# A decoder layer on one core: turned blocks of the feed-forward issued in spaced steps, token-tile differences on GpSimd, attention values one item later, down splits inside the last pair

## The chip, the cores and the metric

The kernel runs on one core of a Trainium2 chip. The time is that of one execution on the device in microseconds (us). The core's engines run side by side, each through its own list of instructions in order: TensorE (PE) multiplies matrices, VectorE (DVE), ScalarE (ACT) and GpSimd (POOL) work on tiles, SyncE (SP) issues transfers. An instruction waits on semaphores for what it needs, and all behind it in its engine's list waits with it.

## The reference

One layer of a decoder over 1024 tokens of width 1024, all in fp32, with three parts, each followed by a layer norm of `ALPHA * x + f(x)`:

```python
h = hybrid_mixer(x, w_in, ml_conv_w, ...)     # mLSTM heads and sliding-window attention, one output projection
x = layer_norm(ALPHA * x + h, ln1_g, ln1_b)
h = memory_cross_attention(x, mem, xa_wq, xa_wkv, xa_wo)    # 4 heads, 256 memory tokens
x = layer_norm(ALPHA * x + h, ln2_g, ln2_b)
u = causal_dwconv(x @ w_up, conv_w, conv_b)                 # width 3
g, val = split(u, 2)
x = layer_norm(ALPHA * x + (gelu(g) * val) @ w_down, ln3_g, ln3_b)   # 2816 inner channels
```

The mixer's query and key channels pass a causal convolution of width 4 and a SiLU before the mLSTM. The sliding-window attention has 8 heads of 64 (4 to a key-value head), a window of 128 tokens, a bias by distance and a sink for each head.

## The kernel before

**Numbers.** Every fp32 operand of a product is held as two parts, a high (`whi`, `aA`, `pt[0]`; a copy that rounds, on ACT) and a low (the difference, on DVE or POOL). `mm3` (L146) makes a product of three matmuls: high times high, high times low, low times high (L147 to L149). Whoever makes the low last holds up the second or third matmul. `hi_lo` (L79) is the pair of copy and subtraction, `stage` (L120) the same for weights.

**Order.** The order on every engine is the order in which the program is written. Side work is written as generators: `also` (L52) opens one, each `yield us` asks to go on that many microseconds later on a clock of its own that `tick` moves by 0.68 us for each `mm3`, and `tick` (L62) issues what is due between two products. So steps of norms, attention and turns lie between the matmuls by these numbers. `drain` (L68) issues all that is left.

**The mixer** runs in two halves of 512 tokens. In each, `swa` (L489) walks 16 items (token tile by pair of heads) as side work of the projections: logits `lg` on PE (L442), bias and maximum on DVE (L450), the exponent on ACT (L458), normalisation on DVE (L467), then `swa_turn` (four transposes on PE into the PSUM tile `tp`, and the pair `pt` by `hi_lo`), then `swa_values` (six matmuls `pv`). Beside it run the projections of `qk`, whose convolution (`qk_steps`, L406) is on DVE too (L418, L424). The PSUM tiles `lg`, `tp`, `pv` come from one pool of 4 buffers, `mx`.

**Cross-attention.** `attend` is the side work for one head beside the next head's query projection (L854).

**The feed-forward** makes the up-projection of 22 pairs of blocks (128 gate and 128 value channels) with seven products P1 to P7 in place of eight, as Strassen does, on blocks of x turned to channels: B11 and B21 (first half of the tokens), B22, and the differences T1 to T4. `column_steps` (L902) works out, for one token tile of each half, norm and differences (L900) and turns them (L893); it runs as side work of the last columns of the `wo` projection and of the first products. `seq` (L944) is the order of the products: P1 and P2 of the first four pairs (they need B11 and B21 alone), then P6, the first that needs a difference. `slot_steps` loads, sums and splits the weight blocks (`block_hi`, `block_lo`) some slots ahead. `gated_steps` does convolution and gate of a pair (L1042 and L1054 on ACT, L1045 and L1057 on DVE) and writes it out on POOL's queue (L1058).

**The down-projection** loads weights and activations on SP's queue (L1135, L1137) and splits them (`down_split`, L1141); its first tiles are made before and between the last two up products.

Of the kernel before, what the change touches and what calls it, by code (L numbers as in the profile page):

```python
# [15 lines left out]
P = 128  # L16
# [12 lines left out]
def decoder_layer_kernel(ctx, tc, t, out):  # L29
# [90 lines left out]
    def stage(n):  # L120
        while nsplit[0] <= min(n, len(plan) - 1):
            i = nsplit[0]
            load(i + 1)
            raw, shape = raws.pop(i)
            w = raw.shape[1]
            _, pool, th, tl = pools.get(plan[i][1], pools["w"])
            hi = pool.tile([P, 1024], F32R, tag=th, name=th)
            lo = pool.tile([P, 1024], F32R, tag=tl, name=tl)
            hi, lo = hi[:, :w], lo[:, :w]
            for c in (slice(0, w // 2), slice(w // 2, w)) if i == 0 else (slice(0, w),):  # L130
                nc.scalar.copy(hi[:, c], raw[:, c])  # L131
            eng = nc.gpsimd if plan[i][0][0] == "w_cm" and plan[i][0][1] >= 5 else nc.vector
            eng.tensor_tensor(lo, in0=raw, in1=hi.bitcast(F32), op=SUB)  # L133
            if len(shape) == 3:
                hi, lo = [v.rearrange("p (a b) -> p a b", a=shape[1]) for v in (hi, lo)]
            ready[i] = (hi, lo)
            nsplit[0] += 1
# [332 lines left out]
    def swa_turn(h, tt, p, kb, L):  # L470
        tp = mx.tile([P, 2, 2, P], F32, tag="mx", name="tp")
        for m in range(kb, 2):
            for b in range(2):
                nc.tensor.transpose(tp[:, m, b, :], L[:, b, m * P:(m + 1) * P], ident)
        pt = [ta.tile([P, 2, 256], F32R, tag=f"pt{v}", name="pt", bufs=1) for v in range(2)]
        tv = tp.rearrange("p m a b -> p m (a b)")
# [12 lines left out]
    def swa(h, swq, us):  # L489
        items = [(h, tt, p) for tt in range(4) for p in (0, 2, 1, 3)]  # L490
        lg, turned = [], None
        for n in range(len(items) + 3):
            if turned:
                swa_values(*turned)
            turned = swa_turn(*lg.pop(0)[:5]) if n > 1 and lg else None
            if n >= len(items):
# [210 lines left out]
    swq = sw_proj(0, x)  # L707
    also(swa(0, swq, 3.35), 1.0)
    qk = qk_proj(0, x)
# [134 lines left out]
    def queries(xT):  # L844
        oT = Split(act2, "B")
        for hd in range(4):
            q2 = []
            for d in range(2):
# [4 lines left out]
                q2.append(q)  # L853
            also(attend(hd, q2, oT, 1.5), 0.7)  # L854
        return oT
# [33 lines left out]

    def turn(src, dst, tt):  # L890
        ps = mx.tile([P, 512], F32, tag="mx", name="tps")
        for k in range(4):
            nc.tensor.transpose(ps[:, k * P:(k + 1) * P], src[:, k * P:(k + 1) * P], ident)  # L893
        c = slice(tt * P, (tt + 1) * P)
        hi_lo(dst[0][:, :, c], dst[1][:, :, c], ps.rearrange("p (k c) -> p k c", k=4))

    K1, K2 = slice(0, 512), slice(512, 1024)

    def sub(dst, x, y):
        nc.vector.tensor_tensor(dst, in0=x, in1=y, op=SUB)  # L900

    def column_steps(tt):  # L902

        ya, yb = y_t[tt], y_t[4 + tt]
        yield from norm_steps(yb, ln, 0, 2.15, 2.6)
        nc.gpsimd.dma_start(x2d[4 + tt], yb)
        yield 3.4
        turn(yb[:, K2], B22, tt)
        yield 1.0
        sub(ya[:, K1], yb[:, K1], ya[:, K1])  # L910
        yield 0.8
        turn(ya[:, K1], T1, tt)
        yield 1.5
        sub(yb[:, K1], yb[:, K1], yb[:, K2])
        sub(yb[:, K2], yb[:, K2], ya[:, K1])
        yield 1.0
        turn(yb[:, K1], T3, tt)
        yield 0.8
        sub(ya[:, K2], ya[:, K2], yb[:, K2])
        turn(yb[:, K2], T2, tt)  # L920
        turned.append(tt)

    def last_cols():
# [3 lines left out]
        for tt in range(4):  # L927
# [11 lines left out]
            add_res(1, tt, 1, pss[tt])  # L939
            also(column_steps(tt))  # L940
            tick(0)
# [5 lines left out]
    for i in range(NFT):  # L947
        seq += [("P1" if i >= NB else "P6", i)]
        if i:
            seq += [("P4", i - 1), ("P3", i - 1)]  # L950
        seq += [("P2", i), ("P6", i)] if i >= NB else []
        seq += [("P5", i), ("P7", i)]
    seq += [("P4", NFT - 1), ("P3", NFT - 1)]
# [12 lines left out]
    for i in range(NFT):  # L966
        n = where["P6" if i < NB else "P1", i] - 4
        loads += [(n, i, "v"), (n, i, "g")]
# [11 lines left out]
    def sums_of(p, i):  # L980

        if p == "P6":
            s = sums[i] = act2.tile([P, 4, 512], F32, tag="B", name="ws")
            sub(s[:, 0], graw[i][:, K1], vraw[i][:, K1])
# [36 lines left out]
    slots = slot_steps()  # L1021
    turned = []
    last_cols()
# [36 lines left out]
    def run_slot(p, i):  # L1060
# [4 lines left out]
        if p == "P1":  # L1065
            st["c1"] = wide()
            st["b"] = bank(mo, "mo")
            product(p, i, st["b"], B11, True)
            nc.scalar.copy(st["c1"][:, K2 if early else K1], st["b"])
        elif p == "P2":  # L1070
# [37 lines left out]
    def last_turns():  # L1108
        for tt in range(4):
            while tt not in turned:  # L1110
                yield 0.7
            turn(y_t[tt][:, K2], T4, tt)
            yield 1.5

    next(slots)
    for n, (p, i) in enumerate(seq[:-2]):
        next(slots)
        if n == 0:
            T4 += parts(act2, "B", 8)
            also(last_turns(), 1.0)  # L1120
        if (p, i) == ("P6", 0):
            drain()
            park = wp.tile([P, 2, D], F32, tag="ln", name="park", bufs=1)
        run_slot(p, i)

# [59 lines left out]

    down_split(1)
    tile_mm(0, 0, (0, 1))
# [140 lines left out]
```

## Time and profile before

| what | value |
|---|---|
| median of 3 runs | 1458.34 us (1458.25 to 1459.07) |
| the profiled execution, its own time | 1457.32 us |
| its span, first to last instruction | 1455.5 us |
| granted TensorE clock, mean | 0.994 of full speed |
| busy: PE, DVE, ACT, POOL | 97%, 68%, 43%, 14% of the span |
| columns of turned blocks and first products, 734 to 800 us | PE busy 77% of the stretch |

A share of busy time is a mean over stages. PE is the bound nearly everywhere; what a stage can still win is its idle time on PE and the stretches in which the granted clock is 0.50 (1.2 in place of 2.4 GHz). In rows of the trace a pair `us, engine line op` gives a start or length, and the part in brackets the idle time before it and what ended it.

### The profile page before, as it was taken

What the parts mean: (1) busy time and instruction counts of PE and PEld (TensorE: products, weight loads), DVE (VectorE), ACT (ScalarE), POOL (GpSimd) and SP (SyncE); (2) the same over time, 40 slices, a digit from 0 to 9 for tenths busy, and PEclk for the clock granted to TensorE, in tenths of its full rate; (3) what the DMA queues carried; (4) which work ended last, traced back from release to release, by engine and by line L of the source; (5) the groups of instructions that cost most, each with busy time, mean ns of one, the idle gap of its engine ahead of it and who ended that gap; (6) DMA issues with size and microseconds to landing.
All of it is one profiled execution on the core that took longest, in us unless ns stands there. A gap on an engine that the chain in (4) does not pass through costs nothing.

```text
span 1455.5 us, 18114 instructions
## 1 busy us (share of the span) xinstructions
PE 1412.2 (97%) x6876; PEld 1169.0 (80%) x6876; DVE 984.0 (68%) x1614; ACT 627.2 (43%) x1079; POOL 197.9 (14%) x258
## 2 busy tenths in 40 slices
PE   9999999999999999999978999999999989999997
PEld 7779888888888978888856788888888868888886
DVE  6587666886675675486586887777777776336535
ACT  6455435564253443234343445544444444323420
POOL 3441014410212010031040000000000000002002
PEclk9999999999999999999999999999999999999999
DMA  7314213124264312232222222221222237525731
GB/s 243 120 48 145 73 53 99 47 78 147 75 219 128 116 58 88 86 116 73 72 101 73 85 90 87 87 83 60 76 87 87 88 115 267 172 83 177 279 94 58
DMA packets 47431, 157.73 MB, mean 108 GB/s; under 512 B 5437, under 2 KB 5845, under 8 KB 46704
## 3 DMA queue, kind: packets, MB, share of 16 engines
q1 hardware_dynamic: 42192, 137.54, 29.1%
q0 software_dynamic: 5152, 19.04, 3.5%
q8 instruction: 54, 0.88, 0.2%
q14 instruction: 33, 0.27, 0.1%
HBM read 136.62 MB, written 21.51 MB: 109 GB/s over the span
## 4 chain that ended last, share of the span: by engine, by line
PE 79%; DVE 13%; ACT 4%; issue 2%; POOL 1%; DMA 0%; SPq 0%; DVEq 0%; ACTq 0%; POOLq 0%
PE upp L147 15%; PE upp L149 15%; PE upp L148 15%; PE ps L149 9%; PE ps L147 9%; PE ps L148 9%; DVE cv L418 3%; DVE L L467 1%; DVE wlo L133 1%; PE tps L235 1%; ACT whi L131 1%; DVE y L228 1%; ACT L L458 1%; DVE L L450 1%; ACT pr L819 1%
## 5 line engine op out<-in xcount | busy, mean ns | idle before, releaser
L147 PE MATMUL upp<-xc,blk 128*128 128x512 f32 x440 | 174.1, 396 | 0.3 <-DVE uc L1036 0.3
L149 PE MATMUL upp<-xc,blk 128*128 128x512 f32 x440 | 174.0, 396 | 0.0
L148 PE MATMUL upp<-xc,blk 128*128 128x512 f32 x440 | 173.7, 395 | 0.0
L133 DVE TENSOR_TENSOR wlo<-raw,whi 128x1024 fp32r<-128x1024 f32 (+2 forms) x97 | 119.3, 1230 | 59.8 <-ACT whi L131 59.5
L131 ACT CAST whi<-raw 128x1024 fp32r<-128x1024 f32 (+3 forms) x114 | 114.2, 1001 | 81.2 <-PE ps L149 66.1
L147 PE MATMUL upp<-dw,ag 128*128 128x512 f32 (+1 forms) x357 | 140.2, 393 | 3.4 <-ACT dw L80 2.1
L148 PE MATMUL upp<-dw,ag 128*128 128x512 f32 (+1 forms) x357 | 139.6, 391 | 2.5 <-DVE dw L81 2.5
L149 PE MATMUL upp<-dw,ag 128*128 128x512 f32 (+1 forms) x357 | 139.5, 391 | 0.0
L147 PE MATMUL ps<-aA,whi 128*128 128x512 f32 x336 | 133.5, 397 | 0.3 <-DVE gat L337 0.3
L149 PE MATMUL ps<-aA,wlo 128*128 128x512 f32 x336 | 131.8, 392 | 0.2 <-POOL wlo L133 0.2
L148 PE MATMUL ps<-aA,whi 128*128 128x512 f32 x336 | 131.2, 390 | 0.0
L1045 DVE SCALAR_TENSOR_TENSOR uc<-uc,fconv 128x1023 f32<-128x1023 f32 x88 | 112.9, 1283 | 26.6 <-ACT uc L1042 25.0
L149 PEld LDWEIGHTS upp<-xc,blk 128*128 128x128 f32 x440 | 82.5, 187 | 20.8 <-DVE blk L900 0.4
L147 PEld LDWEIGHTS upp<-xc,blk 128*128 128x128 f32 x440 | 82.5, 188 | 20.3 <-issue 0.7
L148 PEld LDWEIGHTS upp<-xc,blk 128*128 128x128 f32 x440 | 82.4, 187 | 19.9
L147 PE MATMUL ps<-whi,aA 128*128 128x512 f32 (+2 forms) x256 | 91.4, 357 | 0.2 <-ACT aA L80 0.2
L81 DVE TENSOR_TENSOR ag<-araw,ag 128x512 fp32r<-128x512 f32 x44 | 31.4, 714 | 89.0 <-ACT ag L80 88.9
L149 PE MATMUL ps<-whi,aA 128*128 128x512 f32 (+2 forms) x256 | 89.9, 351 | 0.2 <-DVE aA L81 0.2
L148 PE MATMUL ps<-wlo,aA 128*128 128x512 f32 (+2 forms) x256 | 89.6, 350 | 0.0
L1036 DVE TENSOR_TENSOR uc<-upp,uc 128x512 f32<-128x512 f32 x66 | 45.5, 689 | 62.9 <-PE upp L149 62.8
L147 PEld LDWEIGHTS upp<-dw,ag 128*128 128x128 f32 x357 | 67.3, 188 | 18.8 <-ACT dw L80 2.6
L148 PEld LDWEIGHTS upp<-dw,ag 128*128 128x128 f32 x357 | 67.4, 189 | 18.2 <-DVE dw L81 3.2
(395 smaller groups left out, 3215.3 us busy)
## 6 DMA issues: line engine op xcount, KB each, us to landing
raw<-in_w_up SPq DMA_DIRECT2D x48, 512.0 KB, 3.8
raw<-in_w_down SPq DMA_DIRECT2D x44, 512.0 KB, 4.4
raw<-in_w_cm SPq DMA_DIRECT2D x26, 512.0 KB, 3.7
ad<-uc POOLq DMA_DIRECT2D x22, 512.0 KB, 5.2
araw<-ad SPq DMA_DIRECT2D x44, 256.0 KB, 3.5
raw<-in_w_out SPq DMA_DIRECT2D x16, 512.0 KB, 4.2
raw<-in_wq SPq DMA_DIRECT2D x16, 512.0 KB, 3.6
raw<-in_wo SPq DMA_DIRECT2D x16, 512.0 KB, 3.6
```

The lines of the kernel that those rows point to most:

```text
L81: nc.vector.tensor_tensor(lo, in0=src, in1=hi.bitcast(F32), op=SUB)
L131: nc.scalar.copy(hi[:, c], raw[:, c])
L133: eng.tensor_tensor(lo, in0=raw, in1=hi.bitcast(F32), op=SUB)
L147: nc.tensor.matmul(ps, lhsT=ahi, rhs=bhi, start=start, stop=False, skip_group_check=more)
L148: nc.tensor.matmul(ps, lhsT=ahi, rhs=blo, start=False, stop=False, skip_group_check=more)
L149: nc.tensor.matmul(ps, lhsT=alo, rhs=bhi, start=False, stop=stop, skip_group_check=more)
L228: nc.vector.scalar_tensor_tensor(y, in0=y, scalar=rs[:, 0:1], in1=ln[:, 0, :], op0=MUL, op1=MUL)
L235: nc.tensor.transpose(ps[:, k * P:(k + 1) * P], y[:, kk * P:(kk + 1) * P], ident)
L418: nc.vector.scalar_tensor_tensor(cv, in0=xc[:, j:j + 512], scalar=mlc[:, i, j:j + 1], in1=cv, op0=MUL, op1=ADD)
L450: nc.vector.tensor_tensor_reduce(L[:, b, kb * P:256], in0=lv[:, b, :], in1=btab[:, i, kb * P:], scale=-1.0, scalar=nsnk[:, i:i + 1], op0=A ...
L1036: nc.vector.tensor_tensor(dst, in0=ps, in1=y, op=ADD)
L1045: nc.vector.scalar_tensor_tensor(u[:, d:S], in0=x[:, 0:S - d], scalar=fconv[:, i, 2 - d:3 - d], in1=u[:, d:S], op0=MUL, op1=ADD)
```

## The change

- `stage`: the lows of the 16 qk weight tiles (eight in each half) are made on DVE instead of POOL.
- `swa`: `pt` has two buffers, `turned` holds up to two items, and the values of an item are issued two items behind its turn, not one. The first half's attention starts 1 us later.
- `attend`'s steps are 2.0 us apart instead of 1.5.
- `turn` is a generator: transposes, 0.8 us later ACT's copy, 0.8 us later DVE's subtraction, with at most two open; before, all three were issued together.
- `column_steps`: the four differences of a token tile (16 in all) go from DVE to POOL, the first of them ahead of the turn of B22, and the write of the normed tile `yb` to `x2d` from POOL's queue to SP's.
- A P1 of the first four pairs issues all of that token tile's column steps behind its product, before the copy of its result. P5 of the first pair comes before its P6, and the rest of the column steps before P5, the turns of T4 before P4.
- In the last pair, the first down weights are loaded at P6 and split at P5, the second at P7; before, both were split behind the loop.
- The scratch for descriptors of transfers on POOL's queue is halved.

```diff
-            eng = nc.gpsimd if plan[i][0][0] == "w_cm" and plan[i][0][1] >= 5 else nc.vector
-            eng.tensor_tensor(lo, in0=raw, in1=hi.bitcast(F32), op=SUB)
+            nc.vector.tensor_tensor(lo, in0=raw, in1=hi.bitcast(F32), op=SUB)
...
-        pt = [ta.tile([P, 2, 256], F32R, tag=f"pt{v}", name="pt", bufs=1) for v in range(2)]
+        pt = [ta.tile([P, 2, 256], F32R, tag=f"pt{v}", name="pt", bufs=2) for v in range(2)]
...
-        lg, turned = [], None
-        for n in range(len(items) + 3):
-            if turned:
-                swa_values(*turned)
-            turned = swa_turn(*lg.pop(0)[:5]) if n > 1 and lg else None
+        lg, turned = [], []
+        for n in range(len(items) + 4):
+            if len(turned) == 2 or n == len(items) + 3:
+                swa_values(*turned.pop(0))
+            if n > 1 and lg:
+                turned.append(swa_turn(*lg.pop(0)[:5]))
...
-    also(swa(0, swq, 3.35), 1.0)
+    also(swa(0, swq, 3.35), 2.0)
...
-            also(attend(hd, q2, oT, 1.5), 0.7)
+            also(attend(hd, q2, oT, 2.0), 0.7)
...
-    def turn(src, dst, tt):
+    def turn(src, dst, tt, us=0.8):
+
+        while opened[0] == 2:
+            yield 0.3
+        opened[0] += 1
         ps = mx.tile([P, 512], F32, tag="mx", name="tps")
...
-        hi_lo(dst[0][:, :, c], dst[1][:, :, c], ps.rearrange("p (k c) -> p k c", k=4))
+        pv = ps.rearrange("p (k c) -> p k c", k=4)
+        yield us
+        nc.scalar.copy(dst[0][:, :, c], pv)
+        yield us
+        nc.vector.tensor_tensor(dst[1][:, :, c], in0=pv, in1=dst[0][:, :, c].bitcast(F32), op=SUB)
+        opened[0] -= 1
...
-        nc.gpsimd.dma_start(x2d[4 + tt], yb)
+        sub(ya[:, K1], yb[:, K1], ya[:, K1], nc.gpsimd)
         yield 3.4
-        turn(yb[:, K2], B22, tt)
-        yield 1.0
-        sub(ya[:, K1], yb[:, K1], ya[:, K1])
-        yield 0.8
-        turn(ya[:, K1], T1, tt)
+        nc.sync.dma_start(x2d[4 + tt], yb)
+        yield from turn(yb[:, K2], B22, tt)
+        sub(yb[:, K1], yb[:, K1], yb[:, K2], nc.gpsimd)
+        yield 0.5
+        yield from turn(ya[:, K1], T1, tt)
+        sub(yb[:, K2], yb[:, K2], ya[:, K1], nc.gpsimd)
         yield 1.5
-        sub(yb[:, K1], yb[:, K1], yb[:, K2])
-        sub(yb[:, K2], yb[:, K2], ya[:, K1])
-        yield 1.0
-        turn(yb[:, K1], T3, tt)
-        yield 0.8
-        sub(ya[:, K2], ya[:, K2], yb[:, K2])
-        turn(yb[:, K2], T2, tt)
+        yield from turn(yb[:, K1], T3, tt)
+        sub(ya[:, K2], ya[:, K2], yb[:, K2], nc.gpsimd)
+        yield from turn(yb[:, K2], T2, tt)
...
-            also(column_steps(tt))
+            columns.append(also(column_steps(tt)))
...
-        seq += [("P1" if i >= NB else "P6", i)]
+        seq += [("P1", i)] if i >= NB else [("P5", i), ("P6", i)] if i == 0 else [("P6", i)]
...
-            st["c1"] = wide()
             st["b"] = bank(mo, "mo")
             product(p, i, st["b"], B11, True)
+            if early:
+                drain(columns[i])
+            st["c1"] = wide()
             nc.scalar.copy(st["c1"][:, K2 if early else K1], st["b"])
...
+        if (p, i) == ("P5", 0):
+            drain(*columns)
+        if (p, i) == ("P4", 0):
+            drain(turns)
...
+        if i == NFT - 1 and p in ("P6", "P5", "P7"):
+            down_load(0) if p == "P6" else down_split(0 if p == "P5" else 1)
+
...
-    nc = _bacc.Bacc("TRN2", target_bir_lowering=False, num_devices=1, dynamic_dma_scratch_size=8192)
+    nc = _bacc.Bacc("TRN2", target_bir_lowering=False, num_devices=1, dynamic_dma_scratch_size=4096)
```

How the instructions stand in the engines' lists, at three places (a number behind a name tells one tile from another of that name).

PE in the first half's attention, before. `pt_1272` and `pt_1273` are high and low of the turn made one item earlier:

```order
L147 MATMUL pv_1314<-pt_1272,swv0_111 128x256
L148 MATMUL pv_1314<-pt_1273,swv0_111 128x256
L149 MATMUL pv_1314<-pt_1272,swv1_112 128x256
L474 MATMUL tp_1322<-ident_117,L_1209 128x128 x4
L442 MATMUL lg_1331<-kk0_107,swq_355 128x256
L443 MATMUL lg_1331<-klo0_109,swq_355 128x256
```

The same place after the change, where that turn's pair is called `pt_1271` and `pt_1272`, and `pt_1200` and `pt_1201` are of the turn before it:

```order
L146 MATMUL pv_1312<-pt_1200,swv0_111 128x256
L147 MATMUL pv_1312<-pt_1201,swv0_111 128x256
L148 MATMUL pv_1312<-pt_1200,swv1_112 128x256
L473 MATMUL tp_1320<-ident_117,L_1209 128x128 x4
L441 MATMUL lg_1329<-kk0_107,swq_355 128x256
L442 MATMUL lg_1329<-klo0_109,swq_355 128x256
```

The values read the older pair; transposes and logits behind them stand as they did.

DVE beside the qk projection of the first half, one item and the convolution of one block, before (L424 and L418 are the convolution, L461, L467 and L81 the attention's normalisation and `pt` low):

```order
L424 SCALAR_TENSOR_TENSOR qk<-th,cv 128x512
L461 RECIPROCAL ssum<-ssum 128x2
L467 TENSOR_SCALAR L<-L,ssum 128x128 x2
L418 SCALAR_TENSOR_TENSOR cv<-xc,mlc,cv 128x512 x2
L81 TENSOR_TENSOR pt<-tp,pt 128x256
```

And after, a line lower in the numbers:

```order
L423 SCALAR_TENSOR_TENSOR qk<-th,cv 128x512
L132 TENSOR_TENSOR wlo<-raw,whi 128x1024
L417 SCALAR_TENSOR_TENSOR cv<-xc,mlc,cv 128x512 x2
L460 RECIPROCAL ssum<-ssum 128x2
L466 TENSOR_SCALAR L<-L,ssum 128x128 x2
L417 SCALAR_TENSOR_TENSOR cv<-xc,mlc,cv 128x512
L81 TENSOR_TENSOR pt<-tp,pt 128x256
```

A weight low of 128x1024 has come in ahead of the item's steps.

POOL at the end of the column steps, before (`rs` are steps of the norm, L229 its last step, L906 the write to `x2d`, L1058 that of the gated pairs):

```order
L212 TENSOR_TENSOR rs<-mv,eps_c 128x1
L213 TENSOR_TENSOR rs<-rs,mhalf 128x1
L229 TENSOR_TENSOR y<-y,ln 128x1024
L906 DMA x2d<-y 128x1024
L1058 DMA ad<-uc 128x1024 x22
```

And after, where L228 is the norm's last step and L909 the differences:

```order
L909 TENSOR_TENSOR y<-y 128x512
L211 TENSOR_TENSOR rs<-mv,eps_c 128x1
L212 TENSOR_TENSOR rs<-rs,mhalf 128x1
L909 TENSOR_TENSOR y<-y 128x512 x3
L228 TENSOR_TENSOR y<-y,ln 128x1024
L909 TENSOR_TENSOR y<-y 128x512 x8
L1066 DMA ad<-uc 128x1024 x22
```

Eight of the sixteen differences stand behind the last tile's norm, four between the last two norms; no write to `x2d` is left on this queue here.

## Rows read from the trace of the kernel before

**Rows 1.** The page, busy us of each engine and its share of the span.

```profile
PE 1412.2 (97%) x6876; PEld 1169.0 (80%) x6876; DVE 984.0 (68%) x1614; ACT 627.2 (43%) x1079; POOL 197.9 (14%) x258
```

**Rows 2.** Waits of PE: us in total, times, longest us.

```profile
PE tps L893 <- DVE y L900: 9.4, 4, 4.8
PE pv L148 <- DVE pt L81: 9.2, 10, 1.9
PE upp L147 <- ACT uc L1069: 2.9, 4, 0.8
PE upp L149 <- DVE blk L900: 2.6, 1, 2.6
PE upp L148 <- DVE dw L81: 2.5, 1, 2.5
PE upp L147 <- ACT dw L80: 2.1, 1, 2.1
PE xtp L831 <- DVE pr L825: 1.9, 3, 1.1
```

**Rows 3.** Windows: us; busy PE, PEld, DVE, ACT, POOL; granted clock, DMA share, GB/s.

```profile
40.00:122.00 82.00, 75.40 (x398) 63.70 (x397) 63.28 (x138) 43.62 (x105) 35.44 (x47) 1.00 0.23 71
...
734.00:800.00 66.00, 50.86 (x238) 39.40 (x237) 46.42 (x72) 26.23 (x45) 12.05 (x10) 0.95 0.25 88
```

**Rows 4.** Windows of the three stretches at half clock, columns as above.

```profile
267.00:270.30 3.30, 3.30 (x15) 3.15 (x15) 3.09 (x10) 3.12 (x8) 1.36 (x3) 0.50 0.00 0
...
758.50:765.20 6.70, 5.78 (x17) 4.30 (x17) 3.94 (x7) 1.21 (x3) 0.74 (x2) 0.50 0.20 78
...
1195.40:1198.70 3.30, 2.78 (x7) 2.20 (x8) 2.21 (x3) 0.00 (x0) 0.00 (x0) 0.50 1.01 319
```

**Rows 5.** Timeline, 56 to 75 us: start, length, engine, line, operation.

```profile
60.40 2.39 POOL L133 TENSOR_TENSOR wlo<-raw,whi 128x1024 fp32r<-128x1024 f32 x1
...
60.46 3.67 DVE L418 SCALAR_TENSOR_TENSOR cv<-xc,mlc,cv 128x512 f32<-128x512 f32 x2 [0.46 <-POOL cv L413]
...
64.63 0.75 DVE L418 SCALAR_TENSOR_TENSOR cv<-xc,mlc,cv 128x512 f32<-128x512 f32 x1
```

**Rows 6.** Timeline of DVE, 711 to 714 us: a weight low on DVE.

```profile
712.06 1.23 DVE L133 TENSOR_TENSOR wlo<-raw,whi 128x1024 fp32r<-128x1024 f32 x1 [0.39 <-ACT whi L131]
```

**Rows 7.** Timeline of PE, 291 to 294 us: values, then the next logits.

```profile
292.79 0.38 PE L148 MATMUL pv<-pt,swv 128*128 128x256 f32 x1 [1.10 <-DVE pt L81]
...
293.84 0.36 PE L442 MATMUL lg<-kk,swq 128*128 128x256 f32 x1
```

**Rows 8.** Timeline of PE, 785 to 789 us: the first product of a turned block.

```profile
788.08 0.40 PE L147 MATMUL upp<-xc,blk 128*128 128x512 f32 x1
```

**Rows 9.** Timeline of POOL, 712 to 800 us: norm steps of the columns.

```profile
727.40 2.40 POOL L229 TENSOR_TENSOR y<-y,ln 128x1024 f32<-128x1024 f32 x1 [5.97 <-DVE y L228]
...
730.99 0.56 POOL L213 TENSOR_TENSOR rs<-rs,mhalf 128x1 f32<-128x1 f32 x1
```

**Rows 10.** Groups of POOL by line and form: busy us, mean ns, idle before.

```profile
L632 POOL TENSOR_TENSOR ht<-hn,ht 128x512 f32<-128x512 f32 x8 | 11.3, 1417 | 16.9 <-DVE hn L630 16.9
```

**Rows 11.** Timeline of DVE, 727 to 800 us: two differences.

```profile
732.44 0.68 DVE L900 TENSOR_TENSOR y<-y 128x512 f32<-128x512 f32 x1
...
756.37 2.83 DVE L900 TENSOR_TENSOR y<-y 128x512 f32<-128x512 f32 x1
```

**Rows 12.** Timelines of DVE, ACT and SP, 1170 to 1200 us.

```profile
1172.73 0.43 SPq L1135 DMA_DIRECT2D raw<-in_w_down  x1
...
1187.93 1.23 ACT L1042 ACTIVATE uc<-uc,fconv 128x1024 f32<-128x1024 f32 x1
...
1189.19 2.61 DVE L1045 SCALAR_TENSOR_TENSOR uc<-uc,fconv 128x1023 f32<-128x1023 f32 x2 [1.72 <-ACT uc L1042]
```

**Rows 13.** The tile of the bias table: its transfer's issue, its first reader.

```profile
L450 DVE CUSTOM_DVE_ANT_0 L<-lg,btab,nsnk x64: 343/476/486, 54.9 to 334.2; 128x256 f32<-128x256 f32 x56, 128x128 f32<-128x128 f32 x8
L693 POOL DMA_DIRECT2D btab<-ud x1: 942/942/942, 33.4 to 33.4; - x1
```

More of the change, by code (lines that the diff above doesn't have):

```diff
@@ L894, in turn, with sub @@
         c = slice(tt * P, (tt + 1) * P)
-        hi_lo(dst[0][:, :, c], dst[1][:, :, c], ps.rearrange("p (k c) -> p k c", k=4))
+        pv = ps.rearrange("p (k c) -> p k c", k=4)
[4 more added lines that the diff above has]
+        opened[0] -= 1
     K1, K2 = slice(0, 512), slice(512, 1024)
-    def sub(dst, x, y):
-        nc.vector.tensor_tensor(dst, in0=x, in1=y, op=SUB)
+    def sub(dst, x, y, eng=nc.vector):
+        eng.tensor_tensor(dst, in0=x, in1=y, op=SUB)
     def column_steps(tt):
@@ L951, in decoder_layer_kernel @@
         seq += [("P2", i), ("P6", i)] if i >= NB else []
-        seq += [("P5", i), ("P7", i)]
+        seq += [("P5", i), ("P7", i)] if i else [("P7", i)]
     seq += [("P4", NFT - 1), ("P3", NFT - 1)]
@@ L966, in decoder_layer_kernel @@
     for i in range(NFT):
-        n = where["P6" if i < NB else "P1", i] - 4
+        n = (where["P1", i] if i >= NB else min(where["P5", i], where["P6", i])) - 4
         loads += [(n, i, "v"), (n, i, "g")]
@@ L980, in sums_of @@
     def sums_of(p, i):
+        if p in ("P5", "P6") and i not in sums:
+            sums[i] = act2.tile([P, 4, 512], F32, tag="B", name="ws")
         if p == "P6":
-            s = sums[i] = act2.tile([P, 4, 512], F32, tag="B", name="ws")
+            s = sums[i]
             sub(s[:, 0], graw[i][:, K1], vraw[i][:, K1])
@@ L1021, in decoder_layer_kernel @@
     slots = slot_steps()
-    turned = []
+    turned, columns, opened = [], [], [0]
     last_cols()
@@ L1111, in last_turns @@
                 yield 0.7
[L1112 to L1124, printed above, removed]
+            yield from turn(y_t[tt][:, K2], T4, tt)
+            yield 0.5
     order = [(h, j) for h in range(2) for j in range(NFT)]
@@ L1184, in tile_mm @@
                 down_mm(banks[h, tt, ch], h, j, tt, ch, j == 0, j == NFT - 1)
-    down_split(1)
+    next(slots)
+    for n, (p, i) in enumerate(seq[:-2]):
+        next(slots)
+        if n == 0:
+            T4 += parts(act2, "B", 8)
+            turns = also(last_turns(), 1.0)
+        if (p, i) == ("P5", 0):
+            drain(*columns)
+        if (p, i) == ("P4", 0):
+            drain(turns)
+        if (p, i) == ("P6", 0):
+            park = wp.tile([P, 2, D], F32, tag="ln", name="park", bufs=1)
+        run_slot(p, i)
+        if i == NFT - 1 and p in ("P6", "P5", "P7"):
+            down_load(0) if p == "P6" else down_split(0 if p == "P5" else 1)
     tile_mm(0, 0, (0, 1))
```

## The prediction

> **What bounds the kernel now.** First the page's line of busy time: TensorE (PE) works 1412.2 us [rows 1] of a span of 1455.5. That leaves 43.3 us of idle PE, 1.2 of it ahead of the first matmul and 7.1 behind the last. The change takes no matmul away, so all that it can win lies in the other 35 us, and in what runs at half clock. Next, PE's list of waits [rows 2], which says who ends the idle time: 9.2 us in ten waits of the attention values (`pv`) for the `pt` lows; 9.4, 2.9 and 2.6 us around the column turns; 2.1 and 2.5 us ahead of the first down product; 1.9 us in the cross-attention. Then the windows by stage, to see what else is full there: in the first attention stretch DVE is busy for 63.3 of 82 us, so that a delay on it reaches PE; from 734 to 800 us PE works only 50.9 of 66 us [rows 3]. Last the granted clock: three short windows at 0.50, which is the 1.2 GHz level, each right behind such a wait of PE. What runs in them takes twice its time, so each costs half of PE's busy time there: 3.30/2 = 1.7, 5.78/2 = 2.9 and 2.78/2 = 1.4 us [rows 4].
>
> **The lows of the qk weights (POOL to DVE).** While POOL runs a `wlo` (2.39 us from 60.40), a pair of DVE instructions that starts 0.06 us later takes 3.67 us; a single one of the same kind, later and undisturbed, takes 0.75 [rows 5]. So one of the two waited out the POOL instruction, a loss of up to 2.1 us. The Trainium skill ("SBUF — State Buffer", section "SBUF: two separate sides") says why: DVE and GpSimd share a pair of ports, which an instruction of the one keeps to its end against one of the other with two SBUF inputs; this trace agrees, with 3.67 us for a pair at 0.75 each. After the change the hold is gone, but DVE carries the instruction: 1.23 us [rows 6], some 1.13 net since the next one starts about 0.1 us before its end. Eight per half make 9.0 us; eight holds of 0 to 2.1 us cost it 0 to 16.8. In the middle the two are equal, so I count no gain and no loss of DVE time, but the worst single delay falls from 2.1 to 1.13 us.
>
> **Attention values one item later.** PE does not escape the wait altogether. The next item's logits go to the PSUM buffer of the transposes whose `pt` low the values waited for, so they wait for the same DVE instruction. They stand only the values' other matmuls and four transposes later: 293.84 - 292.79 = 1.05 us [rows 7] for a full item, some 0.5 us for the first four items, which have half the matmuls. What a wait has above that is kept: 0.9 us of the longest, 1.9 [rows 2], and some 3 us of the 9.2 when added up over the ten, if the lows come as late as now. If they come 1 us earlier (2.1 less 1.13) nothing is left; if the new DVE work falls ahead of them where there was no hold, all stays. I take the middle of the first two, 1.5 left: 9.2 - 1.5 = **7.7** gained (0 to 9.2), and the half-clock window behind the longest of these waits, **1.7** (0 to 1.7).
>
> **Cross-attention.** A head's steps come 2.0 instead of 1.5 us apart, so the probabilities, for which PE waits up to 1.1 us [rows 2], have 0.5 us more at each of several steps: **1.6** of 1.9 us (0 to 1.9). The last head then ends closer to the output projection; I count nothing for it.
>
> **The column stretch.** This ends for PE with the first product of a fully turned block, at 788.08 [rows 8]. Of the time before, PE idles 66 - 50.9 = 15.1 us [rows 3] and loses 2.9 to the clock [rows 4], 18.0 together. After the change I leave of it:
> - 2.6 us, the wait for the first split block [rows 2]: what stands ahead of that block on DVE stays.
> - 4.8 us: the four copies of P1 now stand on ACT behind the copy of a turn, and PE must turn first. 1.2 us each, a choice; now they cost 0.7 each (2.9 in four).
> - 1.4 us for turns that find a difference not ready, a choice.
> That is 8.8, and 18.0 - 8.8 = **9.2** is gained; the product starts at 778.9. It supposes that the long waits of turns for `y` go, since a turn no longer stands ahead of products that are ready.
>
> What could hold this up is POOL. Its chain starts at 727.40: four L229 of 2.40, three pairs of small steps, whose longer one takes 0.56 [rows 9] and which I put at 0.84 a pair, and sixteen differences of p us. I add 8 us, a choice: 5 for DVE instructions let in between and for the last write of `yb`, which now stands on SP behind weight loads and must have landed before `yb` is overwritten, and 3 from the last difference through turn, copy and subtraction. So the product starts no earlier than 727.4 + 9.6 + 2.5 + 8 + 16p = 747.5 + 16p. The nearest row is POOL's own 128x512 fp32 instruction of two inputs, 1.42 us in the mean [rows 10]: 770.2, not the bound. POOL is the bound from p = 1.96, and at 2.54 the whole 9.2 is gone. A difference on DVE took 0.68 us alone and 2.83 held by an L229 [rows 11]; I take 1.42 as the same engine, shape and type, and 2.83 as the dear end. The bounds of the term: 18.0 less the 2.6 that stay, 15.4, and at p = 2.83 a product at 792.8, a loss of 4.7.
>
> Against this edit speaks the Trainium skill ("GPSIMD Engine Reference", section "4.1 Engine selection"): an elementwise instruction of two inputs belongs on VectorE, as GpSimd takes about twice the time. That makes p an estimated 1.36 us, by which the sum would be the same: the trace agrees (1.42 against 0.68), and the twofold price is paid on an engine for which PE hardly waits.
>
> **Down.** The first pair's weights are loaded a slot or more ahead (1172.73) but split only behind the last slot. Now their split comes earlier: ACT does both highs right behind L1042 (1187.93 + 1.23 = 1189.2, and 0.5 and 1.05 more: 1190.7, when the last product ends); DVE does both lows behind L1045 (1189.19 + 2.61 = 1191.8, and 0.6 and 1.22 more: 1193.6) [rows 12]. The first matmul, of the highs, then follows at once; the second waits for the low, about 2.6 us in place of 2.1 + 2.5: a gain of 2.0. What is pushed back on DVE by 1.8 us, a block's low and an update of `uc`, is needed behind some three microseconds of down matmuls that cover it; uncovered it would cost those 1.8. Behind one wait instead of two the clock may hold, which is worth 1.4: I take 0.9 of it. **2.9** (0.2 to 6.0, with no wait left).
>
> **At nothing.** Half the DMA scratch: the bias table, fetched by POOL's queue at 33.4 us, is first read at 54.9 [rows 13], a cover of 21.5 us for its landing; what it were later than that it would cost.
>
> **Sum.** 7.7 + 1.7 + 1.6 + 9.2 + 2.9 = 23.1 us. The profiled execution took 1457.3 us, which makes 1434.2; the median of the runs is 1.0 above it: **1435.2 us**.
>
> **Rivals.**
> - *The attention waits stay.* DVE, already 77% busy, gets 9 us more per half, and a `wlo` stands ahead of a `pt` low in most items. For: the order on DVE shows one just so. Against: rows 5, the longer hold ends. 1458.3 - (23.1 - 9.4) = 1444.6. Chance 0.11.
> - *POOL bounds the columns.* The differences wait for DVE's work of two SBUF inputs as DVE waited for POOL's, p near 2.5, the term zero: 1458.3 - 13.9 = 1444.4. The Trainium skill's rule on GpSimd bears on this one: no run here shows p. Chance 0.11; with the rival above, 1453.8, another 0.03.
> - *Slower.* The same mechanism turns the sign when the product starts 13.9 us late, at 802: p = (802 - 747.5)/16 = 3.4. At p = 3.6 it starts at 805.1, 17 us late: 1458.3 - 13.9 + 17 = 1461.4. For: a POOL instruction of 2.4 us holds DVE for 2.1, so the two can lock each other. Against: no DVE instruction there is as long as 2 us. Chance 0.06.
> - *Everything hides.* No attention wait, none in cross-attention, columns 15.4, down 6.0: 1458.3 - 9.2 - 1.7 - 1.9 - 15.4 - 6.0 = 1424.1. Chance 0.04.
> - *It does not do what it says*: the waits only change their names (logits for values, copies for turns), and the time stays at 1458. Chance 0.04.
>
> The forecast has 0.61. Half of each term's distance to its bounds, added in squares, gives it a range of its own from 1432 to 1443; to hold 8 in 10 the range takes in the first two rivals above and as much below, towards the case in which everything hides: **1427 to 1446**. That leaves out 0.17. Less than 0.2%, 2.9 us, can't be told from no change. Faster 0.90, the same 0.04, slower 0.06.
>
> **What would show it.** Right: no wait of `pv` for `pt`, and at most some 1.5 us of `lg` for it; differences on POOL of 1.3 to 1.5 us; no wait of 2 us or more between the first split block and the first product of turned columns, and four short ones for the copies of P1; one wait of some 2.6 us ahead of the down products, for a low on DVE; full clock near 267 and 758 us. Wrong: waits of `lg` of a microsecond and more in many items; PE waiting for POOL's differences; half clock in new places; DVE instructions of 2 us beside POOL's; a new wait between the last head of cross-attention and its output projection.

## The result, and the profile after

The changed kernel took 1440.73 us (median of four, 1437.31 to 1442.26) beside 1458.7 us for the kernel before, timed again with it: the ratio is 0.9871, 95% interval 0.9852 to 0.9891. The forecast was 1435.2 with a range of 1427 to 1446, so the direction and the range held and the gain came out at 18 us instead of 23. The profiled execution took 1440.82 us; its span is 1439.0 and PE is busy 1406.8 us of it.

PE's list of waits in the changed kernel (us in total, times, longest us), to be set beside [rows 2]:

```profile
PE upp L146 <- ACT uc L1079: 8.4, 4, 4.8
PE upp L148 <- DVE blk L909: 3.1, 1, 3.1
PE upp L147 <- DVE dw L81: 3.1, 2, 2.4
PE lg L441 <- DVE pt L81: 2.8, 5, 0.7
PE upp L146 <- DVE park L1044: 0.9, 1, 0.9
PE tps L897 <- POOL y L909: 0.7, 1, 0.7
PE tp L473 <- DVE L L466: 0.7, 2, 0.5
PE xtp L831 <- DVE pr L825: 0.3, 1, 0.3
```

No `pv` waits for a `pt` low any more; the logits do, for 2.8 us where the values waited 9.2, and no stretch at half clock is left near 267 us. The turns' long waits for `y` are gone. But the copy of P1 (`uc`, L1079), for which PE waited 2.9 us in four, now costs 8.4, and one of the four is 4.8 us long. The windows (columns as in [rows 3]) show two of the three stretches at half clock still there:

```profile
40.00:122.00 82.00, 79.36 (x426) 68.71 (x425) 66.29 (x155) 46.42 (x110) 20.25 (x40) 1.00 0.24 75
...
718.00:785.00 67.00, 53.71 (x261) 42.85 (x260) 44.65 (x61) 27.60 (x48) 33.68 (x26) 0.97 0.32 103
739.10:742.50 3.40, 3.40 (x11) 2.74 (x11) 2.48 (x3) 0.87 (x2) 1.01 (x2) 0.50 0.95 277
1179.40:1182.90 3.50, 3.50 (x10) 2.67 (x10) 2.79 (x4) 0.00 (x0) 0.53 (x1) 0.51 0.94 345
```

Where the time came from is read best by the start of one and the same matmul in both traces:

| matmul | before | after | earlier by | gained since the row above |
|---|---|---|---|---|
| first one behind the gates (waits for `gat`) | 18.43 | 19.03 | -0.6 | |
| gates' transpose, end of the first half's attention (L510) | 243.17 | 239.15 | 4.0 | 4.6 |
| first one with `memT`, after the second half's | 472.46 | 463.70 | 8.8 | 4.7 |
| first one with `gr`, last columns of `wo` | 715.84 | 704.20 | 11.6 | 2.9 |
| the one that waits 0.34 us for `uc`, behind the columns | 828.03 | 812.61 | 15.4 | 3.8 |
| the last one that waits for `y`, down | 1446.37 | 1429.61 | 16.8 | 1.3 |

The attention stretches gained 9.4 us, as the sum said; cross-attention 2.9 (1.6 expected); the column stretch 3.8 (9.2 expected); down 1.3: the two waits of 2.14 and 2.45 us at the split became one of 2.42, and 0.7 us were lost again at 1324 us, to a weight low that came after ACT had waited for a transfer.

The prediction measured the columns by another end, the first product of a fully turned block. Its start, behind the start of the first `gr` matmul, is the time to compare. Before, then after:

```profile
715.84 0.39 PE L147 MATMUL ps<-gr,aB 128*128 128x512 f32 x1
788.08 0.40 PE L147 MATMUL upp<-xc,blk 128*128 128x512 f32 x1
```

```profile
704.20 0.40 PE L146 MATMUL ps<-gr,aB 128*128 128x512 f32 x1
771.49 0.40 PE L146 MATMUL upp<-xc,blk 128*128 128x512 f32 x1
```

That is 72.24 and 67.29 us: 4.95 gained. Below, this time is called the column time.

The 4.8 us wait has one place. POOL's timeline in the changed kernel, up to the first P1:

```profile
718.23 1.29 POOL L909 TENSOR_TENSOR y<-y 128x512 f32<-128x512 f32 x1
...
726.21 3.49 POOL L909 TENSOR_TENSOR y<-y 128x512 f32<-128x512 f32 x2
729.66 2.84 POOL L228 TENSOR_TENSOR y<-y,ln 128x1024 f32<-128x1024 f32 x1
732.58 1.64 POOL L909 TENSOR_TENSOR y<-y 128x512 f32<-128x512 f32 x1
...
735.41 4.16 POOL L909 TENSOR_TENSOR y<-y 128x512 f32<-128x512 f32 x3
```

The timeline of all engines there, with ACT's copy and PE behind it:

```profile
738.38 0.59 ACT L1079 COPY uc<-upp 128x512 f32<-128x512 f32 x1 [3.58 <-POOL y L909]
...
739.02 0.72 PE L146 MATMUL upp<-aA,blk 128*128 128x512 f32 x1 [4.84 <-ACT uc L1079]
```

The copy's destination takes the buffer of the normed tile `yb` of the first token tile (both are tiles of one pool of eight), so it must wait until all readers of `yb` are done, and the one that ends last is the fourth difference, `ya -= yb`. It stands on POOL behind a norm step and differences of the tiles that follow. P2 adds to P1's PSUM bank, so PE waits for the copy. The price of a difference was close to what I took:

```profile
L909 POOL TENSOR_TENSOR y<-y 128x512 f32<-128x512 f32 x16 | 23.1, 1459 | 8.3 <-DMA x2d<-y 7.8
```

1.46 us in the mean (1.42 taken). The row also shows POOL waiting 7.8 us for the write of the last tile's `yb`.

### The profile page after: what moved, and what is told of

Read it like the earlier page. It is cut to its first block, busy times and chain, and to the rows that moved or that the text cites. A ratio compares the mean times of both kernels' runs of the same rounds, so it can differ in the third digit from the quotient of the medians.

```text
span 1439.0 us, 18150 instructions
## 1 busy us (share of the span) xinstructions
PE 1406.8 (98%) x6876; PEld 1169.1 (81%) x6876; DVE 977.0 (68%) x1614; ACT 626.8 (44%) x1079; POOL 188.9 (13%) x254
## 5 line engine op out<-in xcount | busy, mean ns | idle before, releaser
L132 DVE TENSOR_TENSOR wlo<-raw,whi 128x1024 fp32r<-128x1024 f32 (+2 forms) x113 | 139.4, 1233 | 59.5 <-ACT whi L131 58.8
L81 DVE TENSOR_TENSOR ag<-araw,ag 128x512 fp32r<-128x512 f32 x44 | 31.4, 713 | 87.8 <-ACT ag L80 87.8
L147 PEld LDWEIGHTS upp<-dw,ag 128*128 128x128 f32 x357 | 67.3, 188 | 18.8 <-DVE dw L81 3.8
```

The costliest lines, as they stand in the source:

```text
L81: nc.vector.tensor_tensor(lo, in0=src, in1=hi.bitcast(F32), op=SUB)
L132: nc.vector.tensor_tensor(lo, in0=raw, in1=hi.bitcast(F32), op=SUB)
L147: nc.tensor.matmul(ps, lhsT=ahi, rhs=blo, start=False, stop=False, skip_group_check=more)
```

## The experiments

Every run was timed against the kernel before on the same chip; the ratios are to that. The changed kernel is at 0.987.

### The changed kernel once more

No edit. 

> The changed kernel itself once more, since its four executions lie 4.9 us apart and those of the kernel before 2.3. If the spread is in the half-clock stretches or in the order in which DVE and POOL take turns, one execution here differs from another in the column stretch (first wait of P2 for the copy, 4.84 us in the trace so far) and nowhere else. If it is in transfers, the waits behind the second half of the down projection differ. Median 1440.7, between 1439 and 1442.

1440.4 us (1439.66 to 1442.01), ratio 0.9870 [0.9857, 0.9884]. In this profiled execution of 1442.0 us the wait for the copy is 2.75 us instead of 4.84, but two windows at half clock lie in the column stretch instead of one:

```profile
732.80:736.20 3.40, 3.40 (x14) 2.81 (x13) 3.33 (x6) 1.63 (x2) 3.32 (x3) 0.50 0.22 30
739.60:743.00 3.40, 2.83 (x7) 2.15 (x8) 2.29 (x4) 1.53 (x3) 1.58 (x1) 0.50 0.35 99
```

From the first `gr` matmul to the wait for `uc` this execution is 0.4 us faster all the same. It had lost 1.7 us before, in the first attention half (L510 starts at 240.86 instead of 239.15), where I had expected no difference. So the spread has more than one source, and a single trace's whole time says little below 2 us. The wait for the first copy belongs to this spread: in the six profiled executions that leave the columns as changed (these two and those of four runs below) it is 4.84, 2.75, 1.63, 4.84, 1.70 and 2.86 us, and the column time is 65.2 to 67.3 us.

### All differences back on DVE

```diff
-        sub(ya[:, K1], yb[:, K1], ya[:, K1], nc.gpsimd)
+        sub(ya[:, K1], yb[:, K1], ya[:, K1])
```

and the same for the other three. 

> All sixteen differences back on DVE, everything else as changed. Theory Q (POOL's queue): the copy of the first P1 takes the buffer of the token tile yb(0), whose last reader is the fourth difference, and that one stands on POOL behind norms and differences of the next two tiles; on DVE the 4.84 us wait falls to about 1.2, the first block's low comes 0.5 to 1 us earlier, and the half-clock window behind goes (1.7): about 1435, and 1434 to 1438. Theory D (DVE is the bound, the reason for moving them): 16 x 0.68 = 10.9 us more on DVE bring back waits of turns and blocks like the 9.4 us of before: 1443 or more.

1448.16 us, ratio 0.9922 [0.9907, 0.9937]: slower, as theory D said, but not for its reason alone. The wait for the first copy did fall to 1.16 us, as theory Q said. The group of the differences on DVE:

```profile
L909 DVE TENSOR_TENSOR y<-y 128x512 f32<-128x512 f32 x16 | 10.9, 684 | 15.4 <-POOL y L228 10.2 <-DMA x2d<-y 5.2
```

The work is 10.9 us, the idle time of DVE in front of it 15.4. In the changed kernel's order the first difference stands right behind the norm, so DVE waits four times for POOL's L228, 2.5 us each, and once 5.2 us for the write of `yb`; blocks and turns stand behind. The idle time in front of these instructions is larger than their work; no run here separates the two.

### Third and fourth difference on DVE

The first two, which have these waits, stay on POOL.

```diff
-        sub(yb[:, K2], yb[:, K2], ya[:, K1], nc.gpsimd)
+        sub(yb[:, K2], yb[:, K2], ya[:, K1])
...
-        sub(ya[:, K2], ya[:, K2], yb[:, K2], nc.gpsimd)
+        sub(ya[:, K2], ya[:, K2], yb[:, K2])
```

> The third and fourth difference of each token tile on DVE, the first two stay on POOL. Theory Q: the fourth no longer stands in POOL's queue, so the 4.84 us wait falls to 1.2 to 2, at half the DVE time of the run with all on DVE: 1435 to 1437. Theory D: no gain, 1440 or more, with PE waiting for turns behind a DVE difference.

1436.92 us, ratio 0.9846 [0.9830, 0.9861]: the time of theory Q, but not its wait. The wait for the copy is 3.8 us here, as the fourth difference now stood on DVE behind two block lows and two turns:

```profile
736.06 0.58 ACT L1079 COPY uc<-upp 128x512 f32<-128x512 f32 x1 [2.50 <-DVE y L909]
```

### Third and fourth side by side

The edit against the run above:

```diff
         sub(yb[:, K2], yb[:, K2], ya[:, K1])
+        sub(ya[:, K2], ya[:, K2], yb[:, K2])
         yield 1.5
         yield from turn(yb[:, K1], T3, tt)
-        sub(ya[:, K2], ya[:, K2], yb[:, K2])
```

> The run with the third and fourth difference on DVE gained 3.8 us on the changed kernel; its copy of the first P1 still waited 3.8 us, for a fourth difference that stood on DVE behind two block lows and two turns. Here the fourth follows the third at once. Theory Q (that buffer's last reader gates the copy): the wait falls to about 1.2, perhaps the half-clock window behind it goes: 1433 to 1435.5. Rival: both differences now stand ahead of the norm and the first block's low, whose wait grows from 2.9 by 0.6 or more, and nothing is gained: 1436.5 or more.

1437.18 us, ratio 0.9848 [0.9831, 0.9864], the same as the run above. PE's waits in the column stretch:

```profile
PE upp L146 <- ACT uc L1079: 4.7, 4, 1.2
PE upp L148 <- DVE blk L909: 3.6, 1, 3.6
```

The wait for the copy is at 1.2 us like the other three, as in the run with all differences on DVE; in every execution with a longer wait so far the copy's idle time ended with a difference. So its cause is settled, the last reader of that buffer. Both things expected came: the wait for the first block's low grew, from 2.9 to 3.6. The rival's time was nearer.

The medians do not tell this run from the one above, but the column time does: 65.07 us there, and here, between these two starts, 62.99:

```profile
704.20 0.40 PE L146 MATMUL ps<-gr,aB 128*128 128x512 f32 x1
767.19 0.39 PE L146 MATMUL upp<-xc,blk 128*128 128x512 f32 x1
```

That is 9.25 us less than before the change, where the sum had 9.2 for this term.

### The lows of the qk weights back on POOL

```diff
-            nc.vector.tensor_tensor(lo, in0=raw, in1=hi.bitcast(F32), op=SUB)
+            eng = nc.gpsimd if plan[i][0][0] == "w_cm" and plan[i][0][1] >= 5 else nc.vector
+            eng.tensor_tensor(lo, in0=raw, in1=hi.bitcast(F32), op=SUB)
```

> The lows of the qk weights back on POOL, the values still two items behind. My sum gave this part no DVE time, and 1.5 us for the shorter single delay: 1441 to 1444, with waits of the logits for the pt low of up to 1 us, some 3 to 5 us in all in both halves together (3.6 now, logits and transposes). Rival: the whole 9.4 us that the attention stretches gained come from POOL no longer holding DVE; then this run loses them: 1448 or more. Other rival: the lows cost DVE more than the holds did, and the run is faster, 1439 or less.

1450.92 us, ratio 0.9951 [0.9934, 0.9968]: ten microseconds slower than the changed kernel, the first rival's time. My sum fell here. PE's waits in the first half's stretch, then in the second's (40 to 122 and 240 to 325 us):

```profile
PE tp L474 <- DVE L L467: 2.9, 4, 1.7
PE ps L149 <- POOL wlo L133: 1.7, 2, 1.1
PE lg L442 <- DVE pt L81: 1.3, 2, 0.7
...
PE lg L442 <- DVE pt L81: 4.3, 5, 1.6
PE tp L474 <- DVE L L467: 0.8, 1, 0.8
```

11 us of waits, no less than the 9.2 and 1 of before, though the values stand an item later: the wait moved to the logits, as I had said, and to the transposes, which need the normalised `L` of the same late DVE; that I had not seen. From the gates to the first `memT` matmul this execution takes 456.0 us, against 454.0 in the kernel before and 444.7 in the changed one: with the lows on POOL the attention stretches gain nothing.

### The values one item behind again

```diff
-            if len(turned) == 2 or n == len(items) + 3:
+            if turned:
                 swa_values(*turned.pop(0))
```

> The lows of the qk weights on DVE as changed, but the values again one item behind their turn. The run with the lows on POOL was 10 us slower than the changed kernel, so my even balance for that part is wrong, and values two items behind are worth nothing by themselves. Theory S (the lows alone make the gain; the values' place shifts a wait by 1.05 us): five waits of the logits (2.8 us in all) grow by some 0.5 to 1 us each and a few new ones come up: 1444 to 1447. Theory N (the place of the values is worth nothing even so): 1440 to 1442. Theory B (it takes both): 1449 or more, no better than the run with the lows on POOL.

1440.19 us, ratio 0.9864 [0.9848, 0.9880]: no difference to the changed kernel, theory N. The values wait 3.7 us in the first half and 0.6 in the second; in the changed kernel logits and transposes together wait 2.6 and 0.9. From the gates to `memT` it takes 445.9 us, between the 444.7 and 446.4 of the changed kernel's two executions.

### The kernel before with the lows on DVE alone

The first edit of the change in the old kernel, nothing else. 

> The kernel before with one part of the change alone: the lows of the qk weights on DVE. Theory A: this part makes the whole gain of the attention stretches, since the changed kernel loses 10 us without it and none without the later values. Then 8 to 10 us faster than the kernel before: 1448 to 1451, the ten waits of the values (9.2 us) down to some 4 us, no half clock near 267 us. Rival: it needs the later values or the later start of the first half beside it, and alone it gives what I had put on it, 0 to 3 us: 1456 or more.

1448.83 us, ratio 0.9927 [0.9915, 0.9940]: 11 us faster than the kernel before, with one line of the change. PE's waits in the first half's stretch:

```profile
PE tp L473 <- ACT xc L409: 1.7, 1, 1.7
PE pv L147 <- DVE pt L81: 1.0, 3, 0.5
```

The ten waits for the `pt` lows are five, 1.6 us with the second half's 0.6, from 9.2; there is no half clock near 267 us. From the gates to `memT` it takes 445.5 us, 8.5 less than before. DVE did not get less to do; its busy time was 984.0 us [rows 1] and is now 984.4:

```profile
PE 1412.8 (98%) x6876; PEld 1170.7 (81%) x6876; DVE 984.4 (68%) x1630; ACT 627.7 (43%) x1079; POOL 166.7 (12%) x242
```

### The down splits late

```diff
-        if i == NFT - 1 and p in ("P6", "P5", "P7"):
-            down_load(0) if p == "P6" else down_split(0 if p == "P5" else 1)
-
+
+    down_split(1)
```

> The first two down splits behind the last slot again, everything else as changed. By the trace of the changed kernel one wait of 2.42 us stands in place of 2.14 + 2.45, and the half-clock window behind it is still there: 2 us slower than the changed kernel, 1442 to 1443.5, with the waits of 2.1 and 2.5 us back. Rival: the cover is gone elsewhere (a block's low pushed back on DVE by 1.8 us), so it makes no difference: 1440 to 1441.

1443.76 us, ratio 0.9898 [0.9879, 0.9917], 3 us slower than the changed kernel. Its waits behind the last slots:

```profile
PE upp L147 <- DVE dw L81: 2.5, 1, 2.5
PE upp L146 <- ACT dw L80: 2.1, 1, 2.1
```

Both are back, against one of 2.42 us in the changed kernel. Its half-clock stretch there lasts longer (1178.2 to 1185.1 us, with 4.49 us of busy PE instead of 3.50), which adds 0.5.

### The writes of the normed tiles on POOL's queue

```diff
-        nc.sync.dma_start(x2d[4 + tt], yb)
+        nc.gpsimd.dma_start(x2d[4 + tt], yb)
```

> The four writes of the normed tile to memory on POOL's queue instead of SP's, at the same place. In the changed kernel the last four differences wait 7.8 us on POOL for the last write, which SP issues at 751.5 behind weight loads. Theory Q: PE sees 0.7 us of that, so 1439.5 to 1441. Rival: POOL's queue frees everything behind it and the turns of the last tile come several us earlier: 1437 or less. Other rival: the issue itself (0.59 us each on POOL) delays the fourth difference of the first tile, and the copy of the first P1 with it: 1442 or more.

1436.86 us, ratio 0.9846 [0.9830, 0.9862]: 4 us faster than the changed kernel, the first rival's time, but only part of its reason. The first line is the changed kernel's wait for these writes, in the list of who waits for the tile `x2d`, the second this run's:

```profile
POOL y L909: 7.8, 1
```

```profile
POOL y L909: 1.1, 1
```

PE's wait for turns of 0.7 us is gone. The wait for the first copy is 2.76 us and the column time 65.8, both within what executions of the changed columns show without this edit. Another 2.4 us of what this execution gained on the profiled one of the changed kernel lie behind the columns: at the down split, where the clock stayed at full this time, behind the same wait of 2.4 us, and at 1324 us (no wait). What these owe to the queue I can't tell from one trace.

### Cross-attention at 1.5 us

```diff
-            also(attend(hd, q2, oT, 2.0), 0.7)
+            also(attend(hd, q2, oT, 1.5), 0.7)
```

> The changed kernel with the steps of cross-attention 1.5 us apart as before. My sum gave the 2.0 us 1.6 us; the same instructions in the two traces came 2.9 us earlier over this stretch. So 1442 to 1443.5, with waits of the transposes for the probabilities of up to 1.1 us back. Rival: what it saves there it gives back as the waits of the last head in the output projection (0.8 us), so 1440.5 to 1441.5.

1442.52 us, ratio 0.9884 [0.9871, 0.9898], some 2 us slower than the changed kernel. From `memT` to `gr` it takes 243.3 us, as before the change (243.4; 240.5 in the changed kernel). The waits are those of [rows 2] again:

```profile
PE xtp L831 <- DVE pr L825: 1.9, 3, 1.1
```

### Both column edits together, and the first block earlier

Third and fourth difference side by side on DVE, and the writes on POOL's queue. 

> Two edits together that were each 3 to 4 us faster than the changed kernel: third and fourth difference side by side on DVE, and the writes of the normed tiles on POOL's queue. Theory Q: the first cuts the wait of the first P1's copy, the second that of the last turns (0.7 to 1 us), and part of the second's gain was that no half-clock window stood behind the down wait in that execution, which does not add up: 1434 to 1437. Rival: they do add up: 1433 or less. Other rival: a write's issue on POOL (0.59 us) holds up the second difference, which the third waits for: 1437 or more.

1435.6 us (1434.19 to 1436.12), ratio 0.9834 [0.9820, 0.9847]: as expected, the two gains overlap: the column time is 63.18 us, no less than the 62.99 with the first edit alone. Then, with these, the steps that split the first weight blocks one pair of triples earlier:

```diff
+                if tt == 3 and j:
+                    next(slots)
                 for kk in range(2):
...
-                if tt == 3 and j:
-                    next(slots)
```

> The run before in this list, with the steps that split the first weight blocks moved ahead of two matmul triples each at the end of the output projection, so that the first block's low stands on DVE ahead of the differences and the norm instead of behind them. The 2.9 to 3.7 us wait for that low is in every run so far and is the one ahead of the half-clock window. Expected: that wait below 1 us and the window gone or late, 1431 to 1434. Rival: the low now waits itself for the weight buffer that the output projection holds, or for its load, and DVE with it: no gain, 1435 or more.

1435.18 us, ratio 0.9839 [0.9826, 0.9852]: the same, so the rival's time, but not its reason. The wait for the first block's low, 3.7 us in the run above, is gone, and PE waits 4.2 us for the copy of P1 again, this time for ACT:

```profile
732.39 1.15 ACT L225 ACTIVATE y<-y,lnm 128x1024 f32<-128x1024 f32 x1 [3.63 <-DVE lnm L223]
733.45 0.57 ACT L901 CAST xc<-tps 128x512 fp32r<-128x512 f32 x1
733.91 0.59 ACT L1079 COPY uc<-upp 128x512 f32<-128x512 f32 x1
```

The copy stands in ACT's list behind the norm of the last token tile (L225), which waits for that tile's statistics on DVE. The stall went to the next chain.

These two are the fastest versions of the study, about 5 us below the changed kernel and 24 below the one before.

## Why the prediction was right, and where it was not

**Attention (7.7 + 1.7 us).** The sum, 9.4, is what the trace gained, but by luck, since its split was wrong. I had given the lows no DVE time and credited most of the gain to the values' later place. The runs say the reverse: the lows alone, in the kernel before, give 11 us by the median and 8.5 in the attention stretches of the trace; the values' place gives nothing with the lows on DVE, and nothing without. The step that failed starts at "in the middle the two are equal, so I count no gain and no loss of DVE time": the balance is even, as said (984.0 and 984.4 us), but that the lows' move gains nothing by itself does not follow, as PE does not wait for a sum. It waits when an instruction that takes long falls ahead of a `pt` low. The convolution's instructions show how much they were held in the first half's stretch, 40 to 122 us, before and then with the lows alone on DVE; the mean falls from 942 to 749 ns:

```profile
L418 DVE SCALAR_TENSOR_TENSOR cv<-xc,mlc,cv 128x512 f32<-128x512 f32 x24 | 22.6, 942 | 2.4 <-POOL cv L413 2.0
```

```profile
L417 DVE SCALAR_TENSOR_TENSOR cv<-xc,mlc,cv 128x512 f32<-128x512 f32 x24 | 18.0, 749 | 1.7 <-POOL cv L412 1.4
```

One such place, in the run with the lows on POOL (timelines of POOL and DVE):

```profile
70.09 2.39 POOL L133 TENSOR_TENSOR wlo<-raw,whi 128x1024 fp32r<-128x1024 f32 x1
...
70.16 3.66 DVE L418 SCALAR_TENSOR_TENSOR cv<-xc,mlc,cv 128x512 f32<-128x512 f32 x2 [0.92 <-POOL cv L413]
```

and in the changed kernel, at the same work (timeline of DVE):

```profile
66.35 1.22 DVE L132 TENSOR_TENSOR wlo<-raw,whi 128x1024 fp32r<-128x1024 f32 x1
68.25 1.54 DVE L417 SCALAR_TENSOR_TENSOR cv<-xc,mlc,cv 128x512 f32<-128x512 f32 x2 [0.68 <-POOL cv L412]
```

On POOL the low stood right behind the step that releases the pair (L413), so the two started together. On DVE it runs ahead of the pair, which waits for that step anyway, and the pair takes 1.54 us instead of 3.66. Whether the shorter hold or the earlier place is worth more is not shown; no run separates them. That the wait would move to the logits was right; it was worth all of what the later place could have given, not a third, and the logits' 2.8 us are more than the 1.5 left in the sum.

**Cross-attention (1.6).** 2.9 by the trace, 2 by the run without it: more than the upper bound of 1.9, and only part of it by the mechanism named. The waits for probabilities fell by the 1.6 us, from 1.9 to 0.3, but the last head's closeness costs 0.8 us of new waits for `pT`, that I had counted at nothing. From `memT` to `gr`, before and after, 1.2 us of the gain are idle time of PE, and 1.7 are busy time for the same 1275 matmuls:

```profile
472.46:715.84 243.38, 241.08 (x1275) 202.61 (x1274) 157.98 (x239) 97.06 (x177) 27.52 (x28) 1.00 0.28 89
```

```profile
463.70:704.20 240.50, 239.40 (x1275) 203.32 (x1274) 156.03 (x239) 97.28 (x177) 27.61 (x28) 1.00 0.29 90
```

Why these are shorter is not shown.

**The column stretch (9.2).** The mis-sized term: 3.8 by the table, 4.95 by the prediction's own end, and 5.0 to 7.0 over the six executions. The long waits of turns went, three of the four copies cost 1.16 to 1.22 us (1.2 taken), the first block's wait stayed (3.1, 2.6 taken). Three things were not in it. The first copy's wait, 1.6 to 4.84 us: I had POOL's chain as a bound for the end of the stretch only, 747.5 + 16p, and it bound the beginning, since the fourth difference of the first tile frees a buffer that P1's copy takes. The half-clock window: I counted all 2.9 us of it as gained, and half of 3.40, 1.7, stayed, with waits of 3 to 5 us left ahead of it. And 0.9 us at a product of the new order, which waits for an update of `park`; this lies behind the prediction's end and is in the 3.8 alone. With the third and fourth difference side by side on DVE the term is 9.25, so the first of these is the larger miss; that this meets the sum is again in part luck, as a half-clock window is left there and no wait for turns, for which the sum had 1.4. The rival in which POOL bounds the columns was half true, by its queue's order and not by p, which came out at 1.46. The spaced turns, the steps issued behind P1 and the new place of P5 were not tried each by itself, so what each gave is not shown.

**Down (2.9).** 2.2 by the waits of the trace: the one left is 2.42 us, near the 2.6 worked out. The half clock behind it, of which 0.9 us was counted as gained, stayed in this execution. By medians the part is worth 3.

**The two rules.** The Trainium skill ("SBUF — State Buffer", section "SBUF: two separate sides") describes an exclusive lock on the ports that DVE and GpSimd share. The trace agrees in the column stretch too, where two differences on POOL took 3.49 us beside DVE instructions of two SBUF inputs, for 1.29 each alone. The Trainium skill's advice to put such instructions on VectorE ("GPSIMD Engine Reference", section "4.1 Engine selection") holds in its price, 1.46 against 0.68 us; by itself it would have put all sixteen on DVE, which costs 7.5 us in the changed order.

**At nothing.** The halved scratch was not tried by itself; no wait in the trace points to it.

## What to carry to other kernels

Two engines that can hold each other should not be given work that becomes ready at the same event: move it, and look at the longest delay in front of the instruction that is waited for, not at the sum of busy time, which was the same here. When work goes to another queue, ask of each piece what it waits for, what buffer its end sets free, and which instruction takes that buffer next: that one is held up, though it uses none of the data. And an instruction moved one step later in a list gained nothing here, where the ones behind it wait for the same producer.

## What the runs showed of the hardware that was not expected

The granted clock does not fall behind every wait of the same length: behind the down split PE waited 2.40 to 2.42 us in eleven of the profiled executions. In eight of them it then ran at 0.50 for 3.4 us; in three it did not (all differences on DVE, the writes on POOL's queue, and that with the third and fourth difference side by side). For the second of these the row shows the full 2.4 GHz:

```profile
1174.00:1181.00 7.00, 4.59 (x20) 3.32 (x19) 6.96 (x9) 2.27 (x4) 0.53 (x1) 1.00 0.71 253
```

Such a stretch costs half of PE's busy time in it, 1.75 us of 3.50 in the changed kernel, and it is a part of the 2 to 5 us by which executions of one kernel differ here. No edit of the study explains when it comes: the last run has its writes on POOL's queue too, and the stretch at half clock.
